# The first two output pairs of a hybrid decoder trunk in turn, both in seven products

## The chip, the cores and the metric

The kernel runs on one core of a Trainium2 chip. The time is that of the device in microseconds for one execution, lower is better. The engines are TensorE (PE; PEld is its weight load), VectorE (DVE), ScalarE (ACT), GpSimd (POOL) and SyncE (SP), which here only issues transfers.

## The reference

One layer over 2048 rows of 1024 numbers and 16 meta rows before them, in float32:

```python
hn = rms_norm(h, norm_g)
cx, cb, cc, cg, q, k, v, rg = jnp.split(hn @ w_in, 8, axis=-1)        # each 512 wide
conv_out = short_conv_branch(cx, cb, cc, conv_w) * jax.nn.silu(cg)     # 3 taps, causal
ret = head_group_norm(retention_chunkwise(rotary(q), rotary(k), v), ret_norm_g)
mixed = jnp.concatenate([conv_out, ret * jax.nn.silu(rg)], axis=-1)    # 1024 wide
h = h + mixed @ w_out
return rms_norm(h, final_g)[:, N_META:]
```

Only the last two lines are touched: the output projection, a product of 2048 x 1024 with 1024 x 1024, the addition of the input row, and the last norm.

## The kernel before, in words

**Three matmuls for one.** Each float32 operand is split in a high part (a rounded copy, made by ScalarE) and a low part (the rest, a subtraction by VectorE): `split`, L109. A product is high x high + high x low + low x high, so each block of 128 x 512 columns by 128 rows of depth costs three matmuls. Tiles wh and wl are the high and low parts of weights (the operand that TensorE loads), mh and ml those of the operand that moves.

**Seven products for eight.** Most projections are done in pairs of row blocks as a 2 x 2 block matrix by a 2 x 2 block matrix, with Strassen's seven products (in Winograd's form) in place of eight: `quad`, L225. The weights' sums are made on GpSimd in `stationary` (L136): four additions and subtractions of 128 x 512, and then seven splits. The moving side's sums were made early, in `prepare`, and stored in a tensor of HBM (`sums_w` for w_out); they are loaded and split again by `prepared` (L210). `m` has the split blocks: m[0], m[1], m[5] are blocks of w_out as they are, m[7] (block b12) is needed by the plain form alone, m[2], m[3], m[4], m[6] are sums. Four 128 x 512 tiles make one m[i]. `quad` runs products 0 to 6; after some of them a copy (ScalarE) of the bank is taken, and a "take" adds bank and copy to the result. One product is 12 matmuls, one quad 84. The plain form, `quad_plain` (L282), has 96.

**The ring.** The weights' parts go through three slots (RING = 3, tags wh and wl): the split for product n waits until product n-3 has been read. The raw blocks live in eight slots (tag ra). Tiles loaded from HBM for other ends (tag g: w, t, yo, z and more) share sixteen. Four PSUM banks (tag pj) hold products, four slots (tag tc) the copies.

**The order.** The program is written in Python without loops on the chip. The order of instructions on each engine is fixed before the run by a planner: at each moment of its own estimated time line it picks, for each engine, the first in program order of those whose inputs are ready. `tc.issue_after(ins)` adds that what is traced within it stands behind `ins` on its engine. On the chip each engine then goes through its list in that order, waiting where an input is late.

**The end of the kernel.** Rows come in two halves (r = 0, 1), each with four retention heads and four conv groups; the last unit is a conv group with a quad of CG and CB. Then L1085 loads and splits all sixteen tiles of w_out (`moving`, m[0], m[1], m[7], m[5]), L1086 loads final_g, and `output` (L872) is called for eight pairs of 128-row blocks:
- pair 0 is plain: four weight blocks split as they are (in the slots of m[3]), then the sums m[2] and m[6] are loaded and split, 96 matmuls, then m[3] and m[4], which were kept in SBUF (`held`);
- pairs 1 to 7 are quads with `stationary`;
- each take adds bank to the row of x (yo, on VectorE, L906), squares it for the norm (ScalarE, L913; one of a pair behind the next product's copy, L909), and for two of four blocks multiplies with final_g on GpSimd (z, L917). The addition of a copied bank to yo (L900) is on GpSimd, for pair 1 on VectorE, with the first one put behind the fifth weight split (`fifth`);
- then the norm's factor (two small operations on VectorE, a power on GpSimd), two multiplications on ScalarE (L938), two on VectorE (L941), and four stores.

Of the kernel before, what the change touches and what calls it, by code (L numbers as in the profile page):

```python
# [8 lines left out]
F32 = mybir.dt.float32  # L9
# [4 lines left out]
ALU = mybir.AluOpType  # L14
# [64 lines left out]
def hybrid_trunk(ctx: ExitStack, tc: tile.TileContext, t, out: bass.AP, chunk_decay):  # L79
# [21 lines left out]
    def gen(name="g"):  # L101
        return sb.tile([P, HB + 16], F32, name=name, tag="g", bufs=GEN)[:, : 2 + HB]
# [1 line left out]
    def brief(name="b"):  # L104
        return sb.tile([P, HB + 128], F32, name=name, tag="b", bufs=BRIEF)[:, :HB]

    lowered, fifth = [None], [None]

    def split(hi, lo, src, scale=None, eng=nc.vector):  # L109

        if scale is None:
            nc.scalar.copy(out=hi, in_=src)  # L112
            lowered[0] = eng.tensor_tensor(out=lo, in0=src, in1=hi.bitcast(F32), op=ALU.subtract)  # L113
            return
        nc.scalar.mul(hi, src, scale)  # L115
        nc.vector.scalar_tensor_tensor(  # L116
            out=lo, in0=src, scalar=scale, in1=hi.bitcast(F32), op0=ALU.mult, op1=ALU.subtract
        )

    def add(eng, out, a, b):  # L120
        eng.tensor_tensor(out=out, in0=a, in1=b, op=ALU.add)  # L121
# [14 lines left out]
    def stationary(blocks):  # L136

        a11, a12, a21, a22 = blocks
        s1 = sb.tile([P, HB], F32, name="sa", tag="ra", bufs=RAW)

        def parts(src):
            hi = sb.tile([P, HB], F32R, name="wh", tag="wh", bufs=RING)
            lo = sb.tile([P, HB], F32R, name="wl", tag="wl", bufs=RING)
            split(hi, lo, src)
            return hi, lo

        w = [parts(a11), parts(a12)]
# [3 lines left out]
        summed[0] = nc.gpsimd.tensor_tensor(out=a12, in0=a12, in1=a11, op=ALU.subtract)  # L151
        w += [parts(a) for a in (a11, s1, a21)]
        fifth[0] = lowered[0]
        return w + [parts(a) for a in (a12, a22)]

    def operand(i, kt):
        slot = B12 if i == 7 else i
# [9 lines left out]
    def moving(load, scale=None, after={}):  # L167


        m = [[] for _ in range(8)]  # L170
        blocks = []
        for j in range(2):
            for half in range(2):
                for kt in range(KH):
                    k = half * KH + kt
                    blocks.append(load(k, j))
                    parts(m, BLOCK[half][j], kt, blocks[-1], scale(k) if scale else None)
                    after.get((j, k), lambda: None)()
        return m, blocks

    def block_sums(b11, b12, b22, b21, t1, t3, f, g, eng=nc.vector):

# [42 lines left out]
    def quad(w, m, take, steps=()):  # L225


        steps = iter(steps)

        def product(i, bank, first):  # L230
            (wh, wl) = w[i]
            for kt in range(KH):
                ks = slice(kt * P, (kt + 1) * P)
                mh, ml = m[i][kt]
                for n, (a, b) in enumerate(((wl, mh), (wh, ml), (wh, mh))):
                    nc.tensor.matmul(  # L236
                        bank, a[:, ks], b, start=first and kt == 0 and n == 0, stop=kt == KH - 1 and n == 2,
                        skip_group_check=not first,
                    )
# [29 lines left out]
        take(1, 0, xb, None)  # L269

    def plain_part(n, load, slot):
        a = sb.tile([P, HB], F32, name="ra", tag="ra", bufs=RAW)
# [5 lines left out]
    def plain_parts(loads, slot=PLAIN_W):  # L278
        w = {n: plain_part(n, loads[n], slot)[1] for n in (0, 2, 1, 3)}
        return [w[n] for n in range(4)]  # L280
# [588 lines left out]
            nc.gpsimd.tensor_copy(out=state[h], in_=states[-1])  # L869
        return blocks  # L870

    def output(pair, m, final_g):  # L872
        d = mixed[pair // 2]
        loads = [
            lambda a, i=i, k=k: nc.sync.dma_start(a.rearrange("p (k c) -> p k c", k=KH), d[pair % 2, i, k])
            for i in range(2)
            for k in range(2)
        ]
# [3 lines left out]
        for i in range(2):  # L882
            for j in range(2):
                y = gen("yo")[:, :HB]
                row = (2 * pair + i) * P
                nc.sync.dma_start(y, x[row : row + P, j * HB : (j + 1) * HB])
                ys[i][j] = y
        last = [None]
        squares = []

        def square():
            while squares:
                squares.pop(0)()

        def take(i, j, pp, c):
            y = ys[i][j]
            if c is not None:

                with tc.issue_after(fifth[0].ins) if pair == 1 and i + j == 0 else nullcontext():
                    add(nc.vector if pair == 1 else nc.gpsimd, y, y, c)  # L900
            junk = sb.tile([P, HB], F32, name="rot", tag="rot", bufs=1)

            cut = 2 if c is None and pair == SEQ // (2 * P) - 1 else 1
            for n in range(cut):
                cs = slice(n * HB // cut, (n + 1) * HB // cut)
                last[0] = nc.vector.tensor_tensor(out=y[:, cs], in0=pp[:, cs], in1=y[:, cs], op=ALU.add)  # L906
                at = ss[:, i, 2 * n : 2 * n + 1] if i != j and n else ss[:, i, j : j + 1]
                if pair and i + j == 0:
                    squares.append(lambda cs=cs, at=at: nc.scalar.activation(  # L909
                        junk[:, cs], y[:, cs], AF.Square, accum_out=at  # L910
                    ))
                else:
                    nc.scalar.activation(junk[:, cs], y[:, cs], AF.Square, accum_out=at)  # L913
            cuts[i] = cut
            if i == j:
                ys[i][j] = gen("z")[:, :HB]
                nc.gpsimd.tensor_tensor(out=ys[i][j], in0=y, in1=final_g[:, j * HB : (j + 1) * HB], op=ALU.mult)  # L917

        if pair == 0:
            w = plain_parts(loads)  # L920
            prepared(m, sums_w, (1, 3))
            quad_plain(w, m, take)
            prepared(m, sums_w, (0, 2), held)
        else:
            quad(stationary(load_raw(loads)), m, take, (idle, idle, square))
        for i in range(2):
            tot = small.tile([P, 1], F32, name="tot", tag="tot")
            add(nc.vector, tot, ss[:, i, 0:1], ss[:, i, 1:2])
            if cuts[i] > 1:
                add(nc.vector, tot, tot, ss[:, i, 2:3])  # L930
            rs = small.tile([P, 1], F32, name="rf", tag="rf")
            rsqrt_mean(rs, tot)
            row = (2 * pair + i) * P
            for j in range(2):
                cs = slice(j * HB, (j + 1) * HB)
                y = ys[i][j]
                if i == j:
                    nc.scalar.mul(y, y, rs)  # L938
                else:
                    with tc.issue_after(last[0].ins):  # L940
                        nc.vector.scalar_tensor_tensor(  # L941
                            out=y, in0=y, scalar=rs, in1=final_g[:, cs], op0=ALU.mult, op1=ALU.mult
                        )
                (nc.scalar if i == j and cuts[i] > 1 else nc.sync).dma_start(out[row : row + P, cs], y)

    nc.scalar.dma_start(gain, t["norm1_g"])

# [180 lines left out]
```

## Time and profile before

Three runs took 868.02, 869.04 and 869.08 us, median 869.04. The profiled execution took 868.33, with a span of 866.5 from its first to its last instruction, at a granted TensorE clock of 0.998.

| | busy us | share of the span | instructions |
|---|---|---|---|
| TensorE matmul | 855.4 | 99% | 4216 |
| weight load (beside it) | 705.1 | 81% | 4216 |
| VectorE | 725.7 | 84% | 1194 |
| ScalarE | 497.8 | 57% | 899 |
| GpSimd | 394.6 | 46% | 286 |

Times in the profile are from the start of the span. A line such as "L113 DVE TENSOR_TENSOR wl<-ra,wh 128x512 ... x1" names the line of the kernel (often that of a helper), the engine, the operation, the tile written, the tiles read and the count; in front stand start and duration in us, behind, in brackets, idle time of the engine and what ended it. Matmuls overlap, so that the duration of one is longer than its distance to the next. The output pairs fill the last fifth of the span, from about 698 us on.

### The profile page before, as it was taken

To read this page: it belongs to the slowest core of one execution; us is meant where nothing else is said; L and a number is where in the kernel's file an instruction comes from. 1 tells how busy PE (TensorE), PEld (TensorE's weight loads), DVE (VectorE), ACT (ScalarE), POOL (GpSimd) and SP (SyncE) were. 2 spreads that over 40 slices of the span, in tenths; PEclk is the share of its full clock that TensorE was granted. 3 is DMA by queue.
4 is the path that set the end of the run, shared out by engine and by line. 5 is a ranking of instruction groups with operands and counts; after the bars stand their busy time and mean duration, and the time that the engine had idled before them with its cause. 6 is when DMAs were issued, how large, how long until landed. Compare 5 with 4: busy or idle time off the path is not lost.

```text
span 866.5 us, 12699 instructions
## 1 busy us (share of the span) xinstructions
PE 855.4 (99%) x4216; PEld 705.1 (81%) x4216; DVE 725.7 (84%) x1194; ACT 497.8 (57%) x899; POOL 394.6 (46%) x286
## 2 busy tenths in 40 slices
PE   9999999999999999999999999999999999999996
PEld 6778888888787778788888888888888888788885
DVE  7899988888988977989789898988767799877663
ACT  8676548384755554948374757544333566545553
POOL 0662332423145554352242323354746555677773
PEclk9999999999999999999999999999999999999999
DMA  9724235454656633845264845646123584555431
GB/s 339 233 79 89 72 85 154 113 149 135 159 169 190 199 98 98 313 149 146 62 158 121 159 134 124 205 113 216 48 78 81 173 326 136 169 165 178 156 134 73
DMA packets 127218, 129.51 MB, mean 149 GB/s; under 512 B 58352, under 2 KB 75568, under 8 KB 127152
## 3 DMA queue, kind: packets, MB, share of 16 engines
q1 hardware_dynamic: 126576, 128.30, 50.0%
q8 instruction: 33, 0.54, 0.3%
q10 hardware_dynamic: 576, 0.40, 0.1%
q14 instruction: 33, 0.27, 0.1%
HBM read 90.91 MB, written 25.17 MB: 134 GB/s over the span
## 4 chain that ended last, share of the span: by engine, by line
PE 78%; DVE 6%; issue 1%; ACT 0%; POOL 0%; POOLq 0%; DVEq 0%
PE pj L236 66%; PE pj L293 5%; PE ms L831 1%; PE ms L820 1%; PE ms L830 1%; PE ms L807 1%; DVE wl L113 1%; PE ms L456 1%; DVE ml L113 1%; DVE ml L116 0%; DVE yo L121 0%; DVE yo L906 0%; DVE yo L941 0%; ACT n L407 0%; DVE tc L121 0%
## 5 line engine op out<-in xcount | busy, mean ns | idle before, releaser
L236 PE MATMUL pj<-mh,wl 128*128 128x512 f32 x1008 | 396.0, 393 | 1.3 <-DVE wl L113 0.7
L236 PE MATMUL pj<-mh,wh 128*128 128x512 f32 x1008 | 393.1, 390 | 0.0
L236 PE MATMUL pj<-ml,wh 128*128 128x512 f32 x1008 | 392.9, 390 | 0.0
L112 ACT CAST wh<-ra 128x512 fp32r<-128x512 f32 x216 | 133.9, 620 | 232.1 <-PE pj L236 193.6
L236 PEld LDWEIGHTS pj<-mh,wl 128*128 128x128 f32 x1008 | 189.3, 188 | 43.1 <-issue 1.5
L113 DVE TENSOR_TENSOR wl<-ra,wh 128x512 fp32r<-128x512 f32 x216 | 192.4, 893 | 36.6 <-ACT wh L112 35.2
L236 PEld LDWEIGHTS pj<-mh,wh 128*128 128x128 f32 x1008 | 189.3, 188 | 39.4
L236 PEld LDWEIGHTS pj<-ml,wh 128*128 128x128 f32 x1008 | 189.3, 188 | 38.1
L121 POOL TENSOR_TENSOR sa<-ra 128x512 f32<-128x512 f32 x36 | 54.1, 1504 | 108.8 <-DMA ra<-in_w_in 50.5
L124 POOL TENSOR_TENSOR ra<-sa,ra 128x512 f32<-128x512 f32 x36 | 51.3, 1424 | 81.8 <-DVE wl L113 79.6
L124 POOL TENSOR_TENSOR ra<-ra 128x512 f32<-128x512 f32 x36 | 59.1, 1641 | 59.2 <-PE ms L456 48.9
L151 POOL TENSOR_TENSOR ra<-ra 128x512 f32<-128x512 f32 x36 | 61.5, 1709 | 47.3 <-issue 35.2
L243 ACT COPY tc<-pj 128x512 f32<-128x512 f32 x108 | 62.6, 580 | 0.1
L293 PE MATMUL pj<-mh,mh 128*128 128x512 f32 x128 | 51.0, 401 | 0.6 <-ACT mh L115 0.6
L293 PE MATMUL pj<-mh,ml 128*128 128x512 f32 x128 | 50.0, 390 | 1.0 <-DVE ml L113 1.0
L293 PE MATMUL pj<-ml,mh 128*128 128x512 f32 x128 | 48.0, 391 | 0.0
L843 POOL TENSOR_TENSOR rp<-rs,neg_half 128x4 f32<-128x4 f32 x16 | 19.4, 1211 | 46.4 <-DVE rs L121 46.2
L596 POOL TENSOR_TENSOR c<-c,rr 128x512 f32<-128x512 f32 x14 | 25.7, 1834 | 22.2 <-DVE c L637 14.1
L906 DVE TENSOR_TENSOR yo<-pj,yo 128x512 f32<-128x512 f32 (+1 forms) x33 | 22.0, 671 | 15.9 <-PE pj L236 8.5
L917 POOL TENSOR_TENSOR z<-yo,final_g 128x512 f32<-128x512 f32 x16 | 26.8, 1674 | 18.6 <-DVE yo L906 18.6
L847 DVE TENSOR_SCALAR pm<-ms,mv,rp 128x128 f32<-128x128 f32 x64 | 21.9, 403 | 11.8 <-POOL rp L843 11.8
L112 ACT CAST wh<-sa 128x512 fp32r<-128x512 f32 x36 | 22.2, 618 | 16.0 <-PE pj L236 15.8
(153 smaller groups left out, 1223.2 us busy)
## 6 DMA issues: line engine op xcount, KB each, us to landing
ra<-in_w_in SPq DMA_DIRECT2D x126, 256.0 KB, 2.9
x<-in_xT SPq DMA_DIRECT2D x48, 256.0 KB, 5.0
w<-in_w_out SPq DMA_DIRECT2D x32, 256.0 KB, 4.7
ra<-mixed SPq DMA_DIRECT2D x32, 256.0 KB, 2.7
yo<-in_x SPq DMA_DIRECT2D x32, 256.0 KB, 4.6
ra<-in_x SPq DMA_DIRECT2D x16, 256.0 KB, 3.3
mixed<-c SPq DMA_DIRECT2D x16, 256.0 KB, 2.5
sums_x<-x SPq DMA_DIRECT2D x16, 256.0 KB, 2.8
```

The costliest lines, as they stand in the source:

```text
L112: nc.scalar.copy(out=hi, in_=src)
L113: lowered[0] = eng.tensor_tensor(out=lo, in0=src, in1=hi.bitcast(F32), op=ALU.subtract)
L121: eng.tensor_tensor(out=out, in0=a, in1=b, op=ALU.add)
L124: eng.tensor_tensor(out=out, in0=a, in1=b, op=ALU.subtract)
L151: summed[0] = nc.gpsimd.tensor_tensor(out=a12, in0=a12, in1=a11, op=ALU.subtract)
L236: nc.tensor.matmul(bank, a[:, ks], b, start=first and kt == 0 and n == 0, stop=kt == KH - 1 and n == 2, skip_group_check=not first,)
L243: copied[0] = nc.scalar.copy(out=c, in_=bank)
L293: nc.tensor.matmul(banks[i], a[:, ks], b, start=half + kt + n == 0, stop=half == 1 and kt == KH - 1 and n == 2,)
L596: eng.tensor_tensor(out=out, in0=a, in1=b, op=ALU.mult)
L847: nc.vector.tensor_scalar(out=y[:, cs], in0=o[:, cs], scalar1=mv[:, c, 0:1], scalar2=rp[:, c, :], op0=ALU.subtract, op1=ALU.mult,)
L906: last[0] = nc.vector.tensor_tensor(out=y[:, cs], in0=pp[:, cs], in1=y[:, cs], op=ALU.add)
L917: nc.gpsimd.tensor_tensor(out=ys[i][j], in0=y, in1=final_g[:, j * HB : (j + 1) * HB], op=ALU.mult)
```

## The change

Pairs 0 and 1 are both computed in seven products, and in turn: product 0 of pair 0, product 0 of pair 1, product 1 of pair 0, and so on (`quads`). Of w_out, b11 and b21 (m[0], m[1]) are loaded and split at the beginning, and b12 not at all; m[2], m[3], m[4], m[5], m[6] follow as five `steps`, one after each of the first five turns (`moving_in_turn`). Each step's splits are put behind the last split that had been traced at the beginning of its turn (`behind`): for m[2] that is pair 1's first weight split, for the others the step before. The weights' parts come from a generator (`stationary_in_turn`): the same four sums, made in place, so that no fifth raw block is used, and the split for product i+1 is traced behind product i. Each pair has two PSUM banks, the second used for product 1, and anew for products 3 and 5. The rows of x for both pairs are fetched in the first step, behind the loads for m[2]. The additions of copied banks are on GpSimd for both pairs, the squares aren't held back in either, and the last norm of both pairs follows behind both quads. Pairs 2 to 7 stay as they were.

```diff
-    lowered, fifth = [None], [None]
+    parted = [None, None]
...
         if scale is None:
-            nc.scalar.copy(out=hi, in_=src)
-            lowered[0] = eng.tensor_tensor(out=lo, in0=src, in1=hi.bitcast(F32), op=ALU.subtract)
+            parted[0] = nc.scalar.copy(out=hi, in_=src)
+            parted[1] = eng.tensor_tensor(out=lo, in0=src, in1=hi.bitcast(F32), op=ALU.subtract)
...
+    def stationary_in_turn(blocks):
...
+        yield parts(a11)
+        add(nc.gpsimd, a21, a21, a22)
+        sub(nc.gpsimd, a11, a21, a11)
+        yield parts(a12)
+        sub(nc.gpsimd, a12, a12, a11)
+        yield parts(a11)
+        yield parts(a21)
+        sub(nc.gpsimd, a21, a22, a11)
+        yield parts(a21)
+        yield parts(a12)
+        yield parts(a22)
...
+    def moving_in_turn(load, scale, sums):
+        m = [[] for _ in range(8)]
+
+        def blocks(half, j):
+            for kt in range(KH):
+                k = half * KH + kt
+                parts(m, BLOCK[half][j], kt, load(k, j), scale(k) if scale else None)
+
+        blocks(0, 0)
+        blocks(1, 0)
+        steps = [
+            lambda: sums(m, 1), lambda: sums(m, 0), lambda: sums(m, 2), lambda: blocks(1, 1), lambda: sums(m, 3),
+        ]
+        return m, steps
...
+    def quads(ws, m, takes, between=()):
+        between = iter(between)
+        ws = [[w, next(w)] for w in ws]
+        banks = [[None, None] for _ in ws]
+        copies = [None for _ in ws]
...
+        for i in range(7):
+            behind = list(parted)
+            for n, take in enumerate(takes):
+                if i < 2:
+                    banks[n][i] = ps_proj()
+                bank = banks[n][1 if i in (1, 3, 5) else 0]
+                product(n, i, bank, i in (0, 1, 3))
+                if i == 0:
+                    copies[n] = copy(bank)
+                elif i == 1:
+                    take(0, 0, bank, copies[n])
+                elif i == 2:
+                    copies[n] = [copy(bank)]
+                elif i == 3:
+                    copies[n].append(copy(bank))
+                elif i == 4:
+                    take(1, 1, bank, copies[n][1])
+                elif i == 5:
+                    take(0, 1, bank, copies[n][0])
+                else:
+                    take(1, 0, bank, None)
+                ws[n][1] = next(ws[n][0], None)
+            with ExitStack() as order:
+                for ins in behind:
+                    order.enter_context(tc.issue_after(ins.ins))
+                next(between, idle)()
...
-                with tc.issue_after(fifth[0].ins) if pair == 1 and i + j == 0 else nullcontext():
-                    add(nc.vector if pair == 1 else nc.gpsimd, y, y, c)
+                add(nc.gpsimd, y, y, c)
...
-                if pair and i + j == 0:
+                if pair > 1 and i + j == 0:
...
-        if pair == 0:
-            w = plain_parts(loads)
-            prepared(m, sums_w, (1, 3))
-            quad_plain(w, m, take)
-            prepared(m, sums_w, (0, 2), held)
-        else:
-            quad(stationary(load_raw(loads)), m, take, (idle, idle, square))
...
+        return loads, fetch, take, square, finish
...
-    m, b = moving(load_w_out)
+    m, in_turn = moving_in_turn(load_w_out, None, lambda m, n: prepared(m, sums_w, (n,), held))
     final_g = row_tile("final_g", 1)
     nc.sync.dma_start(final_g, t["final_g"].partition_broadcast(P))
-    for pair in range(SEQ // (2 * P)):
-        output(pair, m, final_g)
+    first_pairs = [output(pair, final_g) for pair in range(2)]
+
+    def behind_first(sums=in_turn[0]):
+        sums()
+        for _, fetch, *_ in first_pairs:
+            fetch()
+
+    quads(
+        [stationary_in_turn(load_raw(loads)) for loads, *_ in first_pairs], m, [take for _, _, take, *_ in first_pairs],
+        [behind_first] + in_turn[1:],
+    )
+    for *_, finish in first_pairs:
+        finish()
+    for pair in range(2, SEQ // (2 * P)):
+        loads, fetch, take, square, finish = output(pair, final_g)
+        fetch()
+        quad(stationary(load_raw(loads)), m, take, (idle, idle, square))
+        finish()
```

More of the change, by code (lines that the diff above doesn't have):

```diff
@@ L151, in stationary, with parts @@
         summed[0] = nc.gpsimd.tensor_tensor(out=a12, in0=a12, in1=a11, op=ALU.subtract)
-        w += [parts(a) for a in (a11, s1, a21)]
-        fifth[0] = lowered[0]
-        return w + [parts(a) for a in (a12, a22)]
+        return w + [parts(a) for a in (a11, s1, a21, a12, a22)]
+    def stationary_in_turn(blocks):
+        a11, a12, a21, a22 = blocks
+        def parts(src):
+            hi = sb.tile([P, HB], F32R, name="wh", tag="wh", bufs=RING)
+            lo = sb.tile([P, HB], F32R, name="wl", tag="wl", bufs=RING)
+            split(hi, lo, src)
+            return hi, lo
+        yield parts(a11)
[9 more added lines that the diff above has]
+        yield parts(a22)
     def operand(i, kt):
@@ L269, in quad, with product, copy @@
         take(1, 0, xb, None)
+    def quads(ws, m, takes, between=()):
[3 more added lines that the diff above has]
+        copies = [None for _ in ws]
+        def product(n, i, bank, first):
+            w, (wh, wl) = ws[n]
+            for kt in range(KH):
+                ks = slice(kt * P, (kt + 1) * P)
+                mh, ml = m[i][kt]
+                for s, (a, b) in enumerate(((wl, mh), (wh, ml), (wh, mh))):
+                    nc.tensor.matmul(
+                        bank, a[:, ks], b, start=first and kt == 0 and s == 0, stop=kt == KH - 1 and s == 2,
+                        skip_group_check=not first,
+                    )
+        def copy(bank):
+            c = sb.tile([P, HB], F32, name="tc", tag="tc", bufs=COPIES)
+            copied[0] = nc.scalar.copy(out=c, in_=bank)
+            return c
+        for i in range(7):
[24 more added lines that the diff above has]
+                next(between, idle)()
     def plain_part(n, load, slot):
@@ L870, in head, with output @@
         return blocks
-    def output(pair, m, final_g):
+    def output(pair, final_g):
         d = mixed[pair // 2]
@@ L881, in output, with fetch @@
         cuts = [1, 1]
[L882 to L887, printed above, removed]
+        def fetch():
+            for i in range(2):
+                for j in range(2):
+                    y = gen("yo")[:, :HB]
+                    row = (2 * pair + i) * P
+                    nc.sync.dma_start(y, x[row : row + P, j * HB : (j + 1) * HB])
+                    ys[i][j] = y
         last = [None]
@@ new lines, in finish @@
+        def finish():
+            for i in range(2):
+                tot = small.tile([P, 1], F32, name="tot", tag="tot")
+                add(nc.vector, tot, ss[:, i, 0:1], ss[:, i, 1:2])
+                if cuts[i] > 1:
+                    add(nc.vector, tot, tot, ss[:, i, 2:3])
+                rs = small.tile([P, 1], F32, name="rf", tag="rf")
+                rsqrt_mean(rs, tot)
+                row = (2 * pair + i) * P
+                for j in range(2):
+                    cs = slice(j * HB, (j + 1) * HB)
+                    y = ys[i][j]
+                    if i == j:
+                        nc.scalar.mul(y, y, rs)
+                    else:
+                        with tc.issue_after(last[0].ins):
+                            nc.vector.scalar_tensor_tensor(
+                                out=y, in0=y, scalar=rs, in1=final_g[:, cs], op0=ALU.mult, op1=ALU.mult
+                            )
+                    (nc.scalar if i == j and cuts[i] > 1 else nc.sync).dma_start(out[row : row + P, cs], y)
```

20 lines of the change are left out of this document (1 added, 19 removed).

## The prediction

> **What bounds the kernel now.** I read the page first, then the chain that ended last in order of time, then the waits of TensorE around the first two pairs.
>
> ```profile
> span 866.5 us, 12699 instructions
> PE 855.4 (99%) x4216; PEld 705.1 (81%) x4216; DVE 725.7 (84%) x1194; ACT 497.8 (57%) x899; POOL 394.6 (46%) x286
> ```
>
> TensorE is busy for 855.4 of 866.5 us, so a matmul less is worth its pitch, as long as no operand comes late for it.
>
> ```profile
> 389.38 19.04 PE pj L236 x84
> 599.81 98.20 PE pj L236 x432
> 698.01 3.20 PE pj L293 x14
> 701.21 2.72 PE pj L236 x12
> 703.93 0.91 PE pj L293 x4
> 704.84 2.72 PE pj L236 x12
> 707.56 17.02 PE pj L293 x75
> 742.05 117.28 PE pj L236 x516
> ```
>
> The columns are start, duration, engine, tile, line, count. 84 matmuls are the seven products of one quad: 19.04 / 84 = 0.2267 us each, 2.72 us for a product of 12. The plain pair 0 (L293) is mixed with the last two products of the last conv quad, and from 742.05 on TensorE runs without a gap. Between, from 650 to 768 us, its waits come to this (us in total, times, longest):
>
> ```profile
> PE pj L236 <- DVE yo L906: 0.5, 1, 0.5
> ```
>
> So 0.5 us is all that can still be won there beside matmuls. VectorE, by stretches (columns: PE, PEld, DVE, ACT, POOL busy with counts, clock, DMA):
>
> ```profile
> 690.00:705.00 15.00, 15.00 (x68) 12.40 (x67) 15.00 (x24) 12.93 (x25) 7.41 (x3) 1.00 1.05 391
> 705.00:725.00 20.00, 20.00 (x90) 16.57 (x89) 19.66 (x23) 10.10 (x21) 10.69 (x7) 1.00 0.53 181
> 762.00:795.00 33.00, 33.00 (x147) 27.32 (x146) 24.77 (x32) 16.95 (x35) 25.16 (x21) 1.00 0.50 161
> ```
>
> Where the output pairs begin, VectorE is busy for all of 15.00 us and 19.66 of 20: it is the second bound, hidden only because splits run ahead of TensorE. In a later pair it has a quarter free.
>
> **How near the splits already come.** Weight splits go through a ring of three: the split for product n can start when product n-3 is done, and is needed two products, 5.44 us, later. The last conv quad:
>
> ```profile
> 687.22 0.62 ACT L112 CAST wh<-sa 128x512 fp32r<-128x512 f32 x1 [0.59 <-PE pj L236]
> 689.00 0.68 DVE L113 TENSOR_TENSOR wl<-sa,wh 128x512 fp32r<-128x512 f32 x1
> 692.54 0.68 DVE L113 TENSOR_TENSOR wl<-ra,wh 128x512 fp32r<-128x512 f32 x1
> 696.15 0.68 DVE L113 TENSOR_TENSOR wl<-ra,wh 128x512 fp32r<-128x512 f32 x1
> 699.16 0.68 DVE L113 TENSOR_TENSOR wl<-ra,wh 128x512 fp32r<-128x512 f32 x1
> ```
>
> The first slot is free at 687.2, the next ones 2.72 apart (689.9, 692.6, 695.4); the low parts end at 689.68, 693.22, 696.83, 699.84: 2.5, 3.3, 4.2 and 4.4 us after. Each falls back because four or five operand splits go before it. Of 5.44, 1.0 is left. Pair 1 later comes nearer still:
>
> ```profile
> L293 PE MATMUL pj<-ml,mh x128: 388/389/500, 6.3 to 724.8; 128*128 128x512 f32 x128
> 729.14 0.60 ACT L112 CAST wh<-sa 128x512 fp32r<-128x512 f32 x1
> 732.16 0.69 DVE L113 TENSOR_TENSOR wl<-sa,wh 128x512 fp32r<-128x512 f32 x1
> ```
>
> Pair 0 ends with the matmul of about 724.8, so pair 1 starts near 725.0, and its fourth product near 725.0 + 3 x 2.72 = 733.2; its low part, whose slot came free at the end of the first, 727.7, ends at 732.85: 5.1 us after, with 0.35 us to spare.
>
> **The change, part by part.** *Matmuls.* Pair 0 goes from 96 (2 column halves x 2 x 4 x 2 x 3) to 84: 12 x 0.2267 = 2.72 us less, at the place that bounds. Running two quads in turn adds no matmul.
>
> *Splits.* Operands: b12 isn't wanted any more, 28 in place of 32. Weights: 14 in place of 4 + 7. Together 42 for 43, at
>
> ```profile
> 697.35 1.88 DVE L113 TENSOR_TENSOR ml<-ra,mh 128x512 fp32r<-128x512 f32 x3
> 697.88 2.18 ACT L112 CAST mh<-w 128x512 fp32r<-128x512 f32 x4
> ```
>
> (1.88 - 0.68) / 2 = 0.60 us of VectorE each back to back, and 2.18 less one of 0.62, over 3, = 0.52 us of ScalarE. In sum next to nothing; ScalarE has 2 to 10 us free in the stretches above.
>
> *GpSimd* gets pair 0's four sums, pair 0's three additions of a copied bank, and pair 1's three, which VectorE did: ten more operations, at
>
> ```profile
> L121 POOL TENSOR_TENSOR yo<-yo,tc x18: 1277/1309/1772, 749.8 to 852.4; 128x512 f32<-128x512 f32 x18
> L917 POOL TENSOR_TENSOR z<-yo,final_g 128x512 f32<-128x512 f32 x4 | 6.7, 1680 | 12.3 <-DVE yo L906 12.3
> ```
>
> about 1.3 to 1.7 us, some 15 us in 38 us of two pairs. GpSimd has the time (10.69 of 20 busy above). What they cost is VectorE's:
>
> ```profile
> 707.50 1.72 POOL L121 TENSOR_TENSOR sa<-ra 128x512 f32<-128x512 f32 x1 [1.79 <-DMA ra<-mixed]
> 707.39 0.68 DVE L113 TENSOR_TENSOR ml<-w,mh 128x512 fp32r<-128x512 f32 x1
> 707.99 1.78 DVE L113 TENSOR_TENSOR ml<-t,mh 128x512 fp32r<-128x512 f32 x1
> 696.61 4.39 POOL L596 TENSOR_TENSOR c<-c,tc 128x512 f32<-128x512 f32 x1 [4.55 <-ACT tc L622]
> ```
>
> The same split takes 0.68 us alone and 1.78 when GpSimd's sum is under way: 1.10 us is what one GpSimd operation can cost it. The other way round, the product at 696.61 took 4.39 us while VectorE's splits went by at 0.60. [...]
>
> *The step from conv to pairs.* With `behind`, the first sums' splits (m2) wait for pair 1's first weight split, hence for the ring slot that the conv quad's sixth product gives back. The conv quad's last two products no longer have plain matmuls to mix with: counted from the L293 start at 698.01, 24 x 0.2267 ends them at 703.4. So pair 1's slot is free near 700.7, m2's splits start about 701.9, and VectorE has only 8 operand splits (b11, b21) ahead of that, not 16 and more: the conv quad's own weights come earlier than above. Pair 0's product 0 needs m0 and its first weights at 703.4, the latter free to split from 698.0: covered. m2 is then needed at 703.4 + 4 x 2.72 = 714.3, m3 at 719.7, and so on by 5.44.
>
> From 701 on, 20 operand splits can run ahead of those dates, as they do now, in the gaps of a list in which weights come first when they are ready. Over the six products to 717 VectorE then has 20 + 6 splits and 3 other operations, 29 x 0.60 = 17.4 us in 6 x 2.72 = 16.3: 1.1 us of lag. In the same time GpSimd has nine operations (pair 0's first difference, the last conv product, pair 1's sum and difference, two a12 differences, two additions, one gain product). The cost of one to VectorE, bounded by the nearest rows: in 690 to 705, (15.00 - 24 x 0.60) / 3 = 0.2 us; in 705 to 725, (19.66 - 23 x 0.60) / 7 = 0.84. Nine cost 1.8 to 7.6. A weight split that is on time takes 0.52 + 0.68 = 1.2 us, so 5.44 - 1.2 = 4.2 us of lag are free. Stall: 1.1 + 1.8 - 4.2, below 0, to 1.1 + 7.6 - 4.2 = 4.5 us. I take the middle price, 0.52, for seven of the nine, since takes that read PSUM leave GpSimd room for about two: 1.1 + 3.6 - 4.2 = 0.5 us. Without any cover (4.2 gone) it would be 4.7.
>
> *Transfers.* SP's queue at this place now:
>
> ```profile
> 673.32 4.66 SPq L875 DMA_DIRECT2D ra<-mixed  x3
> 684.09 9.69 SPq L427 DMA_DIRECT2D w<-in_w_out  x16
> 694.14 2.35 SPq L886 DMA_DIRECT2D yo<-in_x  x4
> ```
>
> After: 8 of w (4.85 us), final_g, five more ra, 4 of t, 8 of yo at 0.3 to 0.6 each, about 15 us from 684, so the last yo is issued near 699 and used from 706: covered by three products. m5's and m6's loads wait for slots of the 16 shared tiles, which 8 yo fill half; they are needed at 730.6 and 736.0, covered. All 8 ra slots are taken by two pairs; the fourth sum of pair 0 (a22 less a11) gives one back near 717, pair 2's split is needed after 736.
>
> *End of the two pairs.* Both `finish` steps come after pair 1: two more multiplications of VectorE at pair 2's start, in the quarter that it has free there. Nothing. The squares of pair 1 aren't held back any more: ScalarE, nothing.
>
> **Sum.** -2.72 + 0.5 = -2.2 us. The profiled execution took 868.33 (span 866.5 and 1.8 around it), so 866.1 for it; it lay 0.7 under the median of 869.04, so 866.8 by that.
>
> **The rivals.** *The gain is eaten* (0.26). No take makes room, and the nine cost 0.45 to 0.84 each, nearer the stretch 705 to 725, whose mix of splits and sums is most like the new one; TensorE waits 1 to 4.5 us for weight splits of products 1 to 3, at 0.64 each 1.1 + 5.8 - 4.2 = 2.7: 869.0. Against it: before, lag of 5.1 us was borne without a stall.
>
> *The turns are lost* (0.24), slower. GpSimd wins every turn, at 1.10 us: 1.1 + 9 x 1.10 - 4.2 = 6.8 us of waiting, net +4.1, 873.1. The place is the low parts for products 1 to 3 of both pairs, 709 to 725 us; it decides once the nine cost over 0.84 us each, 7.6 together: 1.1 + 7.6 - 4.2 = 4.5, the 2.72 and 1.74 more. For it speak six splits that took 6.39 us, not 3.7, beside three sums:
>
> ```profile
> 714.40 6.39 DVE L113 TENSOR_TENSOR ml<-t,mh 128x512 fp32r<-128x512 f32 x6
> 713.42 1.62 POOL L596 TENSOR_TENSOR c<-c,tc 128x512 f32<-128x512 f32 x1 [2.50 <-ACT tc L622]
> 715.00 1.73 POOL L124 TENSOR_TENSOR ra<-sa,ra 128x512 f32<-128x512 f32 x1
> 716.81 1.62 POOL L151 TENSOR_TENSOR ra<-ra 128x512 f32<-128x512 f32 x1
> ```
>
> (6.39 - 3.7) / 3 = 0.9 each. Against it, the 0.2 of 690 to 705.
>
> *A bank comes back late* (0.08). Product 3 writes the bank of product 1 anew, so it waits for its take, and that for GpSimd's addition, sixth and eighth in GpSimd's list. Starved as at 696.61, at 4 us each, pair 1's addition would end near 726, the take at 727, against 722.4: 4 us lost, net +1.3, 870.3. That needs VectorE to win all turns, then splits come early.
>
> **How the numbers follow.** The forecast has 0.42, the eaten gain 0.26, the late bank 0.08, the lost turns 0.24. A measurement of this kernel tells about 0.2%, 1.74 us, from no change. The first is faster, the next two within, the last slower: 0.42, 0.34, 0.24. The likeliest one's own range is 865.5 (no stall, and the 0.5 us of today gone, with 0.3 for the runs) to 867.3 (1 us of stall); to hold 8 in 10 the range goes up to 872.0, into the lost turns.
>
> **What would show it.** Right: 252 matmuls of the two quads and pair 2's in a row from about 703, TensorE's waits from 700 to 745 below 1 us, VectorE's mean split in there under 0.85 us. Wrong: waits of TensorE on low parts (wl) of several us between 709 and 730; weight splits more than 5.4 us behind their slot; or a wait on a take. If the last conv products wait between 698 and 704, the removed mixing with plain matmuls had a use that I set at nothing.

## The result and the profile after

The changed kernel took 880.6 us (median of four, 879.97 to 881.47), beside 868.86 for the kernel before (median of four, 868.02 to 869.08): a ratio of 1.0129, interval 1.0117 to 1.0142. It is 11.7 us slower. The forecast was 866.8, about 2 us faster than before, so the prediction has the sign wrong. The profiled execution took 880.72 us, its span 12.4 longer than before (878.9 against 866.5).

The page of the changed kernel, span and busy time of each engine:

```profile
span 878.9 us, 12676 instructions
PE 855.6 (97%) x4204; PEld 703.4 (80%) x4204; DVE 727.7 (83%) x1190; ACT 498.9 (57%) x901; POOL 408.3 (46%) x296
```

The 12 matmuls are gone (4204 for 4216), and GpSimd has its ten operations more (296 for 286). TensorE, though, is busy for as long as before (855.6 us), in a longer span. Its waits in the changed kernel from 640 to 780 us (us in total, times, longest):

```profile
PE pj L323 <- DVE wl L113: 9.9, 2, 8.8
PE pj L274 <- DVE wl L113: 1.2, 1, 1.2
PE pj L274 <- DVE yo L997: 0.4, 1, 0.4
```

Before, this list held 0.5 us. Now there are 11.5, and 11.1 of them are for low parts of weights. The longest wait decides. The chain of waits of the changed kernel shows what stands in front of it (start, duration, engine, tile, line, count):

```profile
700.77 5.74 PE pj L274 x24
...
713.05 7.03 DVE ml L113 x8
720.08 0.61 DVE wl L113
...
720.73 10.04 PE pj L323 x36
```

The conv quad ends at 700.77 + 5.74 = 706.5, and with that a slot of the ring is free for pair 0's second weights. TensorE needs them two products later, at about 711.9. ScalarE begins their high part at 711.13, and VectorE's low part ends at 720.7. VectorE's and ScalarE's time lines, and GpSimd's beside them, show where they were (the last fence is GpSimd's):

```profile
704.47 0.87 DVE L113 TENSOR_TENSOR wl<-ra,wh 128x512 fp32r<-128x512 f32 x1
...
706.97 4.09 DVE L113 TENSOR_TENSOR ml<-t,mh 128x512 fp32r<-128x512 f32 x3
710.98 0.68 DVE L726 TENSOR_TENSOR c<-pj,c 128x512 f32<-128x512 f32 x1
711.58 1.55 DVE L113 TENSOR_TENSOR ml<-t,mh 128x512 fp32r<-128x512 f32 x1
713.05 7.03 DVE L113 TENSOR_TENSOR ml<-held,mh 128x512 fp32r<-128x512 f32 x8
720.00 1.88 DVE L113 TENSOR_TENSOR wl<-ra,wh 128x512 fp32r<-128x512 f32 x3
```

```profile
706.43 4.26 ACT L112 CAST mh<-held 128x512 fp32r<-128x512 f32 x8
...
711.13 0.61 ACT L112 CAST wh<-ra 128x512 fp32r<-128x512 f32 x1
```

```profile
707.49 1.31 POOL L121 TENSOR_TENSOR ra<-ra 128x512 f32<-128x512 f32 x1 [0.99 <-DMA ra<-mixed]
708.88 1.63 POOL L124 TENSOR_TENSOR ra<-ra 128x512 f32<-128x512 f32 x1
711.30 1.28 POOL L685 TENSOR_TENSOR c<-c,tc 128x512 f32<-128x512 f32 x1 [0.79 <-ACT tc L711]
712.54 3.38 POOL L121 TENSOR_TENSOR yo<-yo,tc 128x512 f32<-128x512 f32 x2
```

Two things are seen. **The order:** m2 (tile t) and then all eight splits of m3 and m4 (held) stand in the two lists ahead of the three weight splits of 720.00, which TensorE wants first. Nothing in the text of the kernel asks for that: `behind` puts m2 behind pair 1's first weights (704.47), and m3 behind m2, but says nothing of m3 and the second turn's weights. **The price:** from 706.97 to 720.00 VectorE does 13 operations. At 0.60 each they would take 7.8 us; they took 13.0. The 5.2 more fall on the five GpSimd operations shown, 1.04 us for each.

Time by stretches: the whole stretch before and after, and after the long wait (columns: length, then busy time and count of PE, PEld, DVE, ACT, POOL, then granted clock, DMA share and GB/s). The first fence is the kernel before, the second the changed one:

```profile
700.00:740.00 40.00, 40.00 (x178) 33.14 (x177) 38.95 (x50) 22.97 (x46) 20.43 (x14) 1.00 0.55 192
```

```profile
700.00:740.00 40.00, 29.35 (x120) 23.53 (x120) 32.41 (x37) 19.27 (x38) 25.77 (x17) 0.91 0.32 106
720.70:724.20 3.50, 3.47 (x8) 2.77 (x9) 1.18 (x2) 0.00 (x0) 3.44 (x2) 0.52 0.00 0
```

In the same 40 us TensorE has 120 matmuls for 178. VectorE, the supposed second bound, does 37 operations for 50 and is free for 7.6 us: it is late first and idle afterwards. Behind the long wait the granted clock is 0.52 for 3.5 us, which loses 3.5 x 0.48 = 1.7 us more.

One more part lies ahead of all this. The two programs are the same up to the conv quad (the lists of the four computing engines agree up to 694 us), and the same ScalarE operation of it stands at (before, then after):

```profile
684.50 0.62 ACT L112 CAST wh<-ra 128x512 fp32r<-128x512 f32 x1 [2.15 <-PE pj L236]
```

```profile
686.10 0.62 ACT L112 CAST wh<-ra 128x512 fp32r<-128x512 f32 x1 [2.15 <-PE pj L274]
```

These 1.6 us are no work of the change; in the profiles of the experiments below that spot lay anywhere from 684.4 to 687.0. The sum for the span: 11.5 - 0.5 of waits, 1.7 of slow clock, 1.6 from ahead, less 2.7 of matmuls, 11.6 of the 12.4; the rest is in gaps of TensorE too short for the list.

### The profile page after: what moved, and what is told of

Same layout as the page of the kernel before. It is cut to its first block, busy times and chain, and to the rows that moved or that the text cites. A ratio compares the mean times of both kernels' runs of the same rounds, so it can differ in the third digit from the quotient of the medians.

```text
span 878.9 us, 12676 instructions
## 1 busy us (share of the span) xinstructions
PE 855.6 (97%) x4204; PEld 703.4 (80%) x4204; DVE 727.7 (83%) x1190; ACT 498.9 (57%) x901; POOL 408.3 (46%) x296
## 4 chain that ended last, share of the span: by engine, by line
PE 72%; DVE 8%; issue 3%; ACT 1%; POOL 1%; DMA 0%; POOLq 0%; DVEq 0%; ACTq 0%
PE pj L274 60%; PE pj L323 3%; PE pj L382 2%; DVE ml L113 2%; DVE wl L113 2%; PE ms L920 1%; PE ms L909 1%; PE ms L919 1%; PE ms L896 1%; PE ms L545 1%; ACT wh L112 0%; DVE qg L949 0%; POOL yo L121 0%; DVE ml L116 0%; DVE w L124 0%
## 5 line engine op out<-in xcount | busy, mean ns | idle before, releaser
L274 PE MATMUL pj<-mh,wl 128*128 128x512 f32 x980 | 385.4, 393 | 2.6 <-DVE wl L113 2.1
L274 PE MATMUL pj<-mh,wh 128*128 128x512 f32 x980 | 382.2, 390 | 0.0
L274 PE MATMUL pj<-ml,wh 128*128 128x512 f32 x980 | 382.0, 390 | 0.0
L113 DVE TENSOR_TENSOR wl<-ra,wh 128x512 fp32r<-128x512 f32 x224 | 197.8, 887 | 38.2 <-ACT wh L112 37.1
L274 PEld LDWEIGHTS pj<-mh,wh 128*128 128x128 f32 x980 | 184.0, 188 | 38.3
L124 POOL TENSOR_TENSOR ra<-ra 128x512 f32<-128x512 f32 x41 | 67.3, 1644 | 67.5 <-PE ms L545 48.6
L151 POOL TENSOR_TENSOR ra<-ra 128x512 f32<-128x512 f32 x35 | 60.3, 1721 | 48.8 <-issue 38.1
L382 PE MATMUL pj<-mh,mh 128*128 128x512 f32 x96 | 38.5, 401 | 1.6 <-ACT mh L115 0.8
L382 PE MATMUL pj<-mh,ml 128*128 128x512 f32 x96 | 37.5, 391 | 1.0 <-DVE ml L113 1.0
L121 POOL TENSOR_TENSOR yo<-yo,tc 128x512 f32<-128x512 f32 x24 | 36.1, 1513 | 3.5 <-ACT tc L281 2.5
L382 PE MATMUL pj<-ml,mh 128*128 128x512 f32 x96 | 35.7, 392 | 0.0
L323 PE MATMUL pj<-mh,wl 128*128 128x512 f32 x56 | 22.5, 407 | 9.9 <-DVE wl L113 9.9
```

Source lines behind the costliest of these rows:

```text
L113: parted[1] = eng.tensor_tensor(out=lo, in0=src, in1=hi.bitcast(F32), op=ALU.subtract)
L124: eng.tensor_tensor(out=out, in0=a, in1=b, op=ALU.subtract)
L274: nc.tensor.matmul(bank, a[:, ks], b, start=first and kt == 0 and n == 0, stop=kt == KH - 1 and n == 2, skip_group_check=not first,)
L323: nc.tensor.matmul(bank, a[:, ks], b, start=first and kt == 0 and s == 0, stop=kt == KH - 1 and s == 2, skip_group_check=not first,)
L382: nc.tensor.matmul(banks[i], a[:, ks], b, start=half + kt + n == 0, stop=half == 1 and kt == KH - 1 and n == 2,)
```

## The experiments

Times are medians, each beside the kernel before on the same chip. "Net" is the difference of the two.

### The order, repaired

`behind` is taken at the end of a turn, not at its beginning, so that each step's splits stand behind the next turn's weight splits.

```diff
         for i in range(7):
-            behind = list(parted)
             for n, take in enumerate(takes):
...
                 ws[n][1] = next(ws[n][0], None)
+            behind = list(parted)
             with ExitStack() as order:
```

> Each step's splits stand behind the weight splits of the next turn, m2's too; nothing else is changed. Theory of the order (twelve operand splits, m2 to m4, stand ahead of the second turn's weight splits in VectorE's and ScalarE's lists, and TensorE waited 8.8 us for those): the waits on wl between 700 and 745 us fall from 11.1 us to under 1.5, and the time is 866.5 to 869, about that of the kernel before less the 2.7 us of matmuls. Rival, the shared turns (GpSimd's ten more operations hold VectorE up, wherever the splits stand): GpSimd's list is the same, so at least 5 us of waiting stay and the time is 872 or more. Rival, the late first splits (operands for seven products in turn can't be made in time at all): the wait moves from wl to the ml of m2 or m3, and the time stays near 880.

Measured: 877.66 (876.78 to 879.4) beside 869.49, ratio 1.0095 (1.0081 to 1.0109), net +8.2. The 866.5 to 869 of the order alone did not come; the shared turns, with 872 or more and at least 5 us of waiting, did. The order is part of it, and the smaller one alone. Waits, VectorE and GpSimd of this kernel:

```profile
PE pj L323 <- DVE wl L113: 6.0, 2, 3.3
PE pj L274 <- DVE wl L113: 1.8, 1, 1.8
```

```profile
711.67 6.88 DVE L113 TENSOR_TENSOR ml<-t,mh 128x512 fp32r<-128x512 f32 x4
718.47 1.75 DVE L113 TENSOR_TENSOR wl<-ra,wh 128x512 fp32r<-128x512 f32 x1
```

```profile
712.87 1.74 POOL L121 TENSOR_TENSOR yo<-yo,tc 128x512 f32<-128x512 f32 x1
714.57 1.74 POOL L124 TENSOR_TENSOR ra<-ra 128x512 f32<-128x512 f32 x1
716.27 1.73 POOL L121 TENSOR_TENSOR yo<-yo,tc 128x512 f32<-128x512 f32 x1
```

Now only m2's four splits stand ahead of the late weight split, and these four take 6.88 us. The starts of GpSimd's operations lie 1.70 apart, and a split takes 6.88 / 4 = 1.72: one split, one GpSimd operation, in turn, 0.60 + 1.1 us for the two.

In a second form m2 stays where the change has it, and only the later steps go behind the next weights.

```diff
-            behind = list(parted)
+            early = list(parted)
...
+            behind = list(parted) if i else early
```

> As the run with every step behind the next turn's weights, but m2's splits where the change put them (behind pair 1's first weights); only m3, m4, m5 and m6 move. Theory of the order: of the twelve splits ahead of the second turn's weights the four of m2 stay, 2.4 us at 0.60 and up to 2.5 more for GpSimd's turns, against 4.2 us that are free: a wait of 0 to 1.5 us, 866.5 to 869.5. Shared turns: 872 or more.

Measured: 876.22 beside 869.49, ratio 1.0071 (1.0059 to 1.0084), net +6.7, again far from the 866.5 to 869.5 of the order alone. It is 1.4 us faster than the first form, so what the order costs lies in the place of the later steps (of these, m3 and m4 stood ahead of the late weights) and not of m2.

### No queueing at all

```diff
                 ws[n][1] = next(ws[n][0], None)
+            behind = []
             with ExitStack() as order:
```

> The changed kernel without any queueing of the steps' splits: m3's, m4's and m2's go into the gaps from 693 us on, partly ahead of pair 0's first weight splits. Theory of the order: VectorE uses the gaps, so that fewer splits stand between the first and the second turn's weights; the wait of 8.8 us shrinks or moves to the conv quad's last weights and pair 0's first, 2 to 8 us in all: 870 to 878. If the queueing of m2 was right as it is, this is slower than the changed kernel, over 880.

Measured: 877.59 beside 869.49, ratio 1.009 (1.0076 to 1.0104), net +8.1, within the 870 to 878 expected of the order; the longest wait for a low part is 5.1 us. So the queueing as the change has it does not keep the weights ahead, and the kernel is better off without it by about 3.6 us. Queued one step later, as above, it gains little over none as long as GpSimd's share stays.

### GpSimd made small

The sums and additions of the first two pairs are done on 32 of 512 columns, in the change's own order: in the two traces the operations of all four computing engines come in the same sequence, so that only GpSimd's time is changed.

```diff
+CUT = 32
...
-        add(nc.gpsimd, a21, a21, a22)
-        sub(nc.gpsimd, a11, a21, a11)
+        add(nc.gpsimd, a21[:, :CUT], a21[:, :CUT], a22[:, :CUT])
+        sub(nc.gpsimd, a11[:, :CUT], a21[:, :CUT], a11[:, :CUT])
...
-                add(nc.gpsimd, y, y, c)
+                cut = CUT if pair < 2 else HB
+                add(nc.gpsimd, y[:, :cut], y[:, :cut], c[:, :cut])
```

> The changed kernel with the four sums and the additions of copied banks of the first two pairs on 32 of 512 columns on GpSimd (a part of both pairs' sums is left out, so the output isn't the reference's); the lists of the engines are the same. It takes the cost of GpSimd's turns out and leaves the order. Theory of the order: the twelve splits still stand ahead, but take 0.60 each in place of 1.0, so the wait of 8.8 us falls to 3 to 4.5 us, the time to 873 to 876. Shared turns: the waits on wl fall under 1 us, 866 to 868. Neither: about 880.

Measured: 873.31 beside 869.49, ratio 1.0037 (1.0024 to 1.0051), net +3.8. Of this kernel, its VectorE, its longest wait, and a stretch behind that:

```profile
707.03 6.09 DVE L114 TENSOR_TENSOR ml<-held,mh 128x512 fp32r<-128x512 f32 x8
713.04 1.94 DVE L114 TENSOR_TENSOR wl<-ra,wh 128x512 fp32r<-128x512 f32 x3
```

```profile
PE pj L324 <- DVE wl L114: 4.0, 1, 4.0
```

```profile
714.00:719.50 5.50, 5.50 (x14) 4.24 (x15) 1.12 (x3) 0.16 (x1) 1.06 (x2) 0.50 0.32 118
```

The eight splits go in 6.09 us, but still ahead of the weights: 4.0 us of wait are left, in the 3 to 4.5 expected of the order, and the 4.8 that went are about the 5.2 reckoned above for the price. The four us cost more than four: the clock is 0.50 for the next 5.5, 2.7 us.

### Both together

The order repaired and GpSimd made small. Against the order repaired alone, one operation of GpSimd stands elsewhere; the lists of the other engines are the same.

> Both at once: each step's splits stand behind the next turn's weight splits, and the sums and additions of the first two pairs on GpSimd work on 32 of 512 columns (part of both pairs' sums is left out, so the output isn't the reference's). Alone, the one left 877.7, the other 873.3. Theory of two causes (order and GpSimd's turns each eat the 4.2 us that are free; only both together are harmless): waits on wl after 705 us under 1 us, 866 to 869. If a third cause holds TensorE up, such as operands that land late, 871 or more.

Measured: 867.13 beside 869.31, ratio 0.9975 (0.9966 to 0.9985), net -2.2. Waits and stretch of this kernel:

```profile
PE pj L275 <- ACT wh L113: 0.7, 1, 0.7
PE pj L275 <- DVE yo L999: 0.3, 1, 0.3
```

```profile
700.00:740.00 40.00, 40.00 (x178) 33.08 (x177) 32.62 (x48) 26.19 (x54) 18.99 (x22) 1.00 0.54 173
```

No wait for a low part is left and 178 matmuls stand in the stretch, as before. Net by the two causes:

| | GpSimd as in the change | GpSimd small |
|---|---|---|
| change's order | +11.7 | +3.8 |
| weights ahead | +8.2 | -2.2 |

Neither alone is enough. The two steps alone take 3.5 and 7.9, together 13.9: either of them leaves a wait, and behind it a stretch at half the clock, which loses 1.7 us in the changed kernel, about as much with the order repaired and 2.7 with GpSimd small. With both there is none.

### The same work on VectorE

Here the price is paid in another coin, and nothing is left out. Banks are added straight to the row by VectorE, from PSUM, without a copy and without GpSimd; the rows of x are fetched ahead of the steps; and the order is the repaired one. In one kernel the eight sums of weights stay on GpSimd, in the other VectorE does them too.

```diff
                 if i == 0:
-                    copies[n] = copy(bank)
+                    take(0, 0, bank, False)
...
+            if c is False:
+                add(nc.vector, y, pp, y)
+                return
```

> As the run with the sums on VectorE, but with the eight sums on GpSimd as in the change. GpSimd keeps 14 of its 20 operations in the stretch. Theory of two causes: 51 x 0.60 and 14 x 1.1 are 46 us in 40, of which some is hidden behind operations that read PSUM: waits of 2 to 5 us, 869 to 873. If only the additions mattered, 867.

Measured, sums on GpSimd: 873.34 beside 869.31, ratio 1.0048 (1.0035 to 1.0061), net +4.0.

```diff
-        add(nc.gpsimd, a21, a21, a22)
-        sub(nc.gpsimd, a11, a21, a11)
+        add(nc.vector, a21, a21, a22)
+        sub(nc.vector, a11, a21, a11)
```

> Each step's splits behind the next turn's weights; the copies of banks and their additions on GpSimd are gone in the first two pairs, VectorE adds each bank straight to the row of x (six operations that read PSUM more, six copies on ScalarE and six additions on GpSimd less); the two pairs' eight sums are on VectorE; the rows of x are fetched before the steps. Theory of two causes: GpSimd's work from 700 to 740 falls to four products and two of conv's; VectorE has about 59 operations of 0.60 us, 35 us in 40, so the waits on wl after 705 us come to under 1.5 us: 866.5 to 869.5. If VectorE's own load is the bound, waits of 3 us and more stay, over 871.

Measured, sums on VectorE: 869.15 beside 869.31, ratio 0.9999 (0.999 to 1.0008), net -0.2. Waits with the sums on GpSimd and a row of VectorE in that kernel; then, with the sums on VectorE, waits, the same row and a row of GpSimd beside it:

```profile
PE pj L323 <- DVE wl L113: 3.4, 3, 1.3
PE pj L274 <- DVE wl L113: 1.7, 1, 1.7
```

```profile
695.13 4.09 DVE L113 TENSOR_TENSOR ml<-w,mh 128x512 fp32r<-128x512 f32 x3
```

```profile
PE pj L323 <- DVE wl L113: 1.1, 3, 0.7
```

```profile
697.37 1.88 DVE L113 TENSOR_TENSOR ml<-w,mh 128x512 fp32r<-128x512 f32 x3
698.27 4.55 POOL L685 TENSOR_TENSOR c<-c,tc 128x512 f32<-128x512 f32 x1 [4.98 <-ACT tc L711]
```

Eight more operations for the engine that is late make the kernel 4.2 us faster: a sum costs VectorE 0.60 us when VectorE does it and about 1.1 when GpSimd does, and 8 x 0.5 is 4.0. The wait of 1.7 in the conv quad goes with them. Ahead of it, three splits had taken 4.09 us beside one of GpSimd's sums and a product of the conv branch (c). With that sum gone it is the product that waits, for 4.55 us, and the three splits take 1.88.

### b21 later

The kernel with everything on VectorE, and m[1]'s splits put behind the conv quad's last weight split.

```diff
+        ahead = list(parted)
         blocks(0, 0)
-        blocks(1, 0)
+        with ExitStack() as order:
+            for ins in ahead:
+                order.enter_context(tc.issue_after(ins.ins))
+            blocks(1, 0)
```

> As the run with direct additions and sums on VectorE, and m1's four splits are put behind the conv quad's last weight split. In the changed kernel TensorE waited 1.3 us before the conv quad's sixth product, because VectorE's splits of m0 and m1 stood ahead of its weights. Theory: that wait goes, 1.0 to 2.0 us faster than without it, 865.5 to 868. If that wait has another cause it stays.

Measured: 869.49 beside 869.31, ratio 0.9999 (0.999 to 1.0008), no difference, and not the 865.5 to 868 expected. The wait that this was to remove, 1.2 us in the changed kernel, was already gone in the kernel that it starts from, so the run doesn't test its cause. What its trace shows beside is SP's queue:

```profile
723.50 11.83 SPq L968 DMA_DIRECT2D ra<-mixed  x5
735.74 1.83 SPq L259 DMA_DIRECT2D t<-sums_w  x4
```

The four loads of m6 stand behind five raw blocks of pair 2, which wait for their slots for 11.83 us.

### A version that beats both

To that kernel two edits: the products with final_g of pairs 0 and 1 go from GpSimd to the last norm on VectorE, and pair 2's raw loads go behind m6's.

```diff
-            if i == j:
+            if i == j and pair > 1:
                 ys[i][j] = gen("z")[:, :HB]
...
-        quad(stationary(load_raw(loads)), m, take, (idle, idle, square))
+        with tc.issue_after(loaded[0].ins) if pair == 2 else nullcontext():
+            raws = load_raw(loads)
+        quad(stationary(raws), m, take, (idle, idle, square))
```

> As the run with m1 late, direct additions and sums on VectorE (869.5; waits on wl of 1.2 us, gaps of 0.4 to 0.8 us between 715 and 741). Two more edits: the product with final_g of the first two pairs isn't made on GpSimd while the quads run, VectorE makes it in the last norm (four operations of GpSimd less there, four of VectorE more behind pair 1), and pair 2's weight blocks are loaded behind the sums for m6 (those loads stood behind five loads that waited 11.8 us for slots). Theory of two causes: four times 1.1 us of VectorE come free between 716 and 738; the remaining waits go to under 0.8 us in all: 866 to 868, faster than the kernel before by 1.5 to 3 us. If VectorE's own load is the bound, no change, about 869.5.

Measured: 867.29 (866.59 to 867.83, eleven runs) beside 869.05, ratio 0.998 (0.9972 to 0.9989), net -1.8: faster than the kernel before and the changed one. Its only wait from 640 to 780, and its stretch:

```profile
PE pj L278 <- DVE wl L113: 0.6, 1, 0.6
```

```profile
700.00:740.00 40.00, 39.90 (x176) 32.65 (x175) 39.69 (x62) 23.05 (x46) 6.71 (x5) 1.00 0.58 181
```

VectorE is busy for 39.69 of 40 us and next to nothing is late. GpSimd's operations in this stretch, with the repaired order: 17 (net +8.2, 27.86 us busy), 14 (+4.0), 9 (-0.2), 5 (-1.8). The two edits weren't run apart.

### Not in turn

Pair 0's quad whole, then pair 1's, each in seven products; the steps go with the first.

```diff
-    quads(
-        [stationary_in_turn(load_raw(loads)) for loads, *_ in first_pairs], m, [take for _, _, take, *_ in first_pairs],
-        [behind_first] + in_turn[1:],
-    )
+    for n, (loads, _, take, *_) in enumerate(first_pairs):
+        quads([stationary_in_turn(load_raw(loads))], m, [take], () if n else [behind_first] + in_turn[1:])
```

> The changed kernel with pair 0's quad first and pair 1's behind it, in place of product by product in turn; the steps go between pair 0's products. Theory of two causes: each m has to be made in 2.72 us where the two pairs in turn give 5.44, four splits and a weight split are 3.0 us at 0.60, more beside GpSimd; the splits of m2 to m4 stand ahead of the second weights again: waits of 10 to 16 us, 880 to 888. If running in turn is what costs, 870 or less.

Measured: 881.02 beside 869.05, ratio 1.0138 (1.0123 to 1.0154), net +12.0. Its waits, and the end of VectorE's list ahead of the longest one:

```profile
PE pj L323 <- DVE wl L113: 9.9, 3, 8.7
PE pj L274 <- ACT mh L112: 1.8, 1, 1.8
```

```profile
712.09 4.37 DVE L113 TENSOR_TENSOR ml<-held,mh 128x512 fp32r<-128x512 f32 x4
716.38 2.96 DVE L113 TENSOR_TENSOR wl<-ra,wh 128x512 fp32r<-128x512 f32 x3
```

The same picture: held splits, then three weight splits, and 8.7 us of wait. With each m needed 2.72 us apart, and not 5.44, it is no worse than the change, so as long as both causes stand, going in turn is neither the cause nor a cure. Whether it matters once they are gone wasn't run.

## Why the prediction was wrong

**The matmuls: right.** 12 x 0.2267 = 2.72 us was the gain to be had. With both causes gone the net is -2.2, with all of the work done -1.8.

**Splits 42 for 43, squares, both ends after pair 1: right** as far as seen; TensorE's wait for a take at pair 2 is 0.4, where pair 1 had 0.5 before.

**The step that failed** is "from 701 on, 20 operand splits can run ahead of those dates ... in the gaps of a list in which weights come first when they are ready". They ran ahead, but ahead of the weights. I took a planner's list for a queue that sorts itself on the chip. Its order is fixed before the run, and twelve operand splits stood in front of weights whose slot was free. The 4.2 us of cover (a split on time 1.2 of 5.44) then meant nothing: the second turn's low part came 720.7 - 706.5 = 14.2 us behind its slot. I had named the test, a weight split more than 5.4 us behind its slot, but had no rival for it. Why the planner put them there wasn't found; it is open.

**The size that was off** is GpSimd's price. I took 0.52 us, the middle of 0.2 and 0.84; here it is 1.04, and 1.1 with the order repaired. The row that said so was in my own text (1.10 for one operation, 0.9 beside three sums), and I gave more weight to whole stretches, in which GpSimd stands still for about half the time (busy for 7.41 of 15 us and 10.69 of 20). No run shows the room for two of the nine operations that takes reading PSUM were to leave; in the changed kernel the five operations shown cost VectorE 5.2 us.

**The rival of the lost turns** (0.24) had the place, 709 to 725 us, the tile and the mechanism. It gave 6.8 us of waiting at 1.10; with the order repaired, TensorE waits 6.0 + 1.8, against 0.7 with GpSimd small as well, 7.1 more. It gave a net of +4.1, though, and +8.2 came: waits of 7.8 for 6.8 are 1.0 of the difference and the clock behind one of them (below) 1.7, the rest I can't divide. The order makes it +11.7.

**The step from conv to pairs: set at nothing, wrong.** TensorE waits 1.2 us for the conv quad's weights. But the missing plain matmuls aren't what that wait hangs on: it is gone when VectorE does the sums, and 1.7 when GpSimd does them. With GpSimd small, 0.7 is left, for a high part.

**Transfers: half right.** x's rows were in time. m6's loads stood in SP's queue behind pair 2's raw blocks, which took 12.90 us there (731.89 to 744.79 in the changed kernel). The prediction doesn't have that order, but TensorE's list of waits has none for them.

**The eaten gain and the late bank** did not come; no wait on a take stands between the products of the two pairs.

## What to carry to other kernels

Where a list is fixed ahead of the run, read the list: "it can run ahead" holds for what stands in front, and a stall is reckoned from the work that stands before the wanted operation. Price an operation of GpSimd by what it costs VectorE (here 1.04 to 1.1 us) and not by GpSimd's free time; where VectorE would do it in 0.60, moving it to the busier engine can be the faster way (873.34 to 869.15 us here). A wait of TensorE of some us is to be counted with the slow matmuls that can follow it (1.7 to 2.7 us here), and not by its length alone.

## What was not expected of the hardware

**One wait, paid twice.** Behind some waits TensorE ran at half its clock (0.50 granted). In the kernel with the order repaired, two waits and the stretches behind them:

```profile
720.27 0.50 PE L323 MATMUL pj<-mh,wl 128*128 128x512 f32 x1 [2.75 <-DVE wl L113]
...
736.35 0.50 PE L323 MATMUL pj<-mh,wl 128*128 128x512 f32 x1 [3.26 <-DVE wl L113]
```

Behind the 2.75 us the clock fell to half, behind the 3.26 it stayed at 1.00, so length alone doesn't decide. The half rate lasts from 721.01 to 724.42 here, 3.41 us; in the changed kernel from 717.25 to 724.08, 6.83 us, of which the first 3.48 lie in the wait itself. Time cut into stretches of 3.41 us from 721.01 on, forward and back, looks so (columns as in the stretches above: behind the length stands TensorE's busy time, behind GpSimd's count the clock):

```profile
717.60:721.01 3.41, 0.74 (x3) 0.65 (x4) 3.41 (x4) 1.60 (x4) 2.18 (x3) 1.00 0.00 0
721.01:724.42 3.41, 3.41 (x9) 2.65 (x9) 3.41 (x5) 1.08 (x3) 1.57 (x1) 0.50 0.00 0
...
731.24:734.65 3.41, 1.85 (x9) 1.19 (x7) 3.41 (x4) 2.22 (x5) 3.41 (x3) 1.00 0.22 77
734.65:738.06 3.41, 1.71 (x7) 1.42 (x8) 3.41 (x3) 1.48 (x3) 2.79 (x2) 1.00 0.20 40
```

The wait of 2.75 us falls into one stretch and leaves 0.74 us of work in it; the next stretch runs at half rate, which loses 1.7 us. The wait of 3.26 is shared out between two, with 1.85 and 1.71 us of work, and nothing falls. In the changed kernel and the runs with the later steps alone repaired, without queueing, with GpSimd small and not in turn, the stretch of 3.41 us ahead of the drop has 0.00 to 0.77 us of work, and none with 1.51 or more was followed by a drop. What decides whether the clock falls wasn't tested.

**Turn by turn, but not always.** With the order repaired, VectorE and GpSimd, both with work at hand, took turns operation by operation, 1.72 us for the two, so that the one whose operation is short paid most: a split of 0.60 took 1.72, nearly three times as long. The other outcome is in the traces too: GpSimd's product took 4.39 us before the change, and 4.55 with the sums on VectorE, while splits went by at 0.60. What decides between the two wasn't tested.
